# An attention stage put in a fixed order on every engine, with its low parts on GpSimd, its row sums shared with VectorE in PSUM, and its gates and reciprocals taken in at the output chunks

## The chip, the core and the metric

The kernel runs on one core of one Trainium2 chip. The core has TensorE (PE, matrix products, which write PSUM), VectorE (DVE), ScalarE (ACT), GpSimd (POOL, which does not touch PSUM here) and SyncE (SP, whose queue issues nearly all DMAs). Each engine works through its own queue in order and waits on semaphores for the others. The metric is the time of one execution in microseconds (us) on the device; lower is better.

## What is computed

One encoder layer on x of 2048 x 1024 in float32. One projection of x is split between two groups of heads.

```python
h = x @ w_in
g_q, g_k, g_v, g_gate, g_lr_f, g_lr_b, m_cq, m_ckv, m_kr, m_gate = split(h)
o_a = gla_branch(...)                 # 4 heads, gated linear attention, both directions, RMSNorm, * silu(g_gate)
q  = rms_norm(m_cq) @ w_uq            # 4 heads, 128 plain + 64 rotary dims
kv = rms_norm(m_ckv) @ w_ukv          # 4 heads, 128 key dims + 128 value dims, from a latent of 128
s  = (q_nope . k_nope + rope(q_rope) . rope(m_kr)) / sqrt(192)
o_b = softmax(s) @ v * silu(m_gate)   # every query against all 2048 keys
x  = layer_norm(2 ** 0.25 * x + concat(o_a, o_b) @ w_out)
```

## The kernel before, in words

**Precision.** Most products keep near-float32 accuracy by splitting each operand into a high part (float32r, written by a copy on ACT, `hi`, L62) and a low part (operand minus high part, on DVE or GpSimd, `lo`, L69). `mm3` (L80) then takes three matmuls: high x high, high x low, low x high. A plain float32 product is one `matmul` in the source and takes several passes on PE.

**Stages.** `sweep_a` (L304) runs over 16 chunks of 128 rows backwards: the projection for the linear attention, and its backward state. It also makes the tables of the rotary angles, `cos` and `sin`, which lie in the constant pool (L172, L173). `late_gates` (L585) loads the weights of the second sweep, and `sweep_c` (L611) runs over the chunks forwards: the forward state, the latent queries, keys and values, the gates. `setup_q` (L209) also scales the value weights `wv` there. Results that the attention needs go to scratch in DRAM: queries (`qa_s`, `qr_s`), gates (`gm_s`), the linear attention's output (`oa_s`).

**The attention** (`attention`, L894) works in latent space. It loops over 16 blocks (4 ranges of 512 queries x 4 heads), and in a block over 8 pairs of key tiles of 128. A step t of the loop handles the scores of pair t and the values of pair t - 11 (`LEAD` = 3 plus the 8 pairs of a block):

- `s_pair` (L929): ten matmuls put the scores of a pair (two tiles of 128 keys x 512 queries) into a PSUM buffer `pS` of two banks; there are two such buffers. ACT copies them to SBUF (L943), DVE takes the running maximum `rm` over 1024 columns (L948).
- `maxima` (L951), once per block: DVE joins the two halves of `rm`, PE transposes them (`mx`), DVE reduces (`mc`), and PE transposes the result back, spread over 128 rows (`mb`).
- `pv_pair` (L967): DVE subtracts the maximum (L970), ACT takes the exponential (L971), GpSimd adds it to the running sum `acc` (L984), and the values are multiplied into `o`. `PV_MODE` (L46) says how for each of the 8 pairs: `d` makes the low part `pl` on DVE, `p` on GpSimd, `n` takes a plain float32 product with the unsplit values `vf` (L988). A block is `dpdpndpd`; the last two blocks have modes of their own (L47).
- `finish` (L1000): the sum is transposed (`sx`), reduced and inverted on DVE, transposed back (`r`, L1017), multiplied into the output (L1018), the product with `wv` is taken in plain float32 (`y`, L1021), the gate is multiplied in (L1023), and the result goes to scratch `ob_s`.

Buffers are handed out in rings (`tile_pool`), and the framework's list scheduler decides in which order each engine's queue holds the instructions, by priorities from the order in the source.

**The output** (`OutProj`, L1085): `load` (L1107) fetches a chunk of 128 rows of both groups' outputs and splits it (high on ACT, low on GpSimd), 16 x 3 x 2 matmuls per chunk against the split `w_out`, then residual and layer norm on DVE. Chunks 0 and 1 run piecewise (`part`) among the last values; chunks 2 to 15 follow, back to back.

Of the kernel before, what the change touches and what calls it, by code (L numbers as in the profile page):

```python
# [39 lines left out]
W_POOL = (3, 5)  # L40
RND = 1.5 * 2.0 ** 23

PV_MODE = "dpdpndpd"  # L46
PV_LAST = {14: "ddpdnddd", 15: "ddddnddd"}  # L47
# [9 lines left out]
class K:  # L57
# [15 lines left out]
    def after(self, *ins):  # L73

        s = ExitStack()
        for i in ins:
            s.enter_context(self.tc.issue_after(i))
        return s

# [71 lines left out]
    def run(self):  # L151
        tc, nc, ins = self.tc, self.nc, self.ins
        with ExitStack() as top:
# [10 lines left out]
            self.oa_s = [dp.tile([P, H, P], F32, name=f"oa_s{c}") for c in range(NCH)]  # L164
            self.ob_s = [dp.tile([P, H, QB], F32, name=f"ob_s{b}") for b in range(NQB)]
# [5 lines left out]
            self.wv = cp.tile([P, H * P], F32, name="wv")  # L171
            self.cos = cp.tile([P, NCH, 32], F32, name="cosT")  # L172
            self.sin = cp.tile([P, NCH, 2, 32], F32, name="sinT")  # L173
# [27 lines left out]
            self.vf = {k: rp.tile([P, P], F32, name=f"vf{k}") for k in range(NKT) if PV_MODE[k // 2] == "n"}  # L201
# [7 lines left out]
    def setup_q(self, w1, ps):  # L209
# [15 lines left out]
        nc.sync.dma_start(self.wv, ins["wv"])  # L225
# [18 lines left out]
        nc.scalar.activation(self.wv, self.wv, AF.Copy, scale=self.gkv_c[:, 0:1])  # L244
# [48 lines left out]

    def rope_tables(self, hpi):
# [6 lines left out]
        V.tensor_scalar(self.sin[:, :, 0, :], self.sin[:, :, 1, :], -1.0, None, ALU.mult)  # L301


    def sweep_a(self):  # L304
        tc, nc, ins, cp = self.tc, self.nc, self.ins, self.cp
        with ExitStack() as ctx:
# [16 lines left out]
            hpi = wp.tile([P, 1], F32, name="hpi")  # L323
            nc.scalar.preload_act_table_set(EXP_LN)
# [260 lines left out]
    def late_gates(self):  # L585

        tc, nc, ins, bc = self.tc, self.nc, self.ins, self.bc
        self.xch = bc.tile([P, NK, 2, P], F32R, name="xch")
# [229 lines left out]
    def ml_norm(self, d, pm):  # L818
# [12 lines left out]
        ckv = self.vf[c] if c in self.vf else w1.tile([P, P], F32, tag="ckv", name=f"ckv{c}")  # L831
# [6 lines left out]
        if c not in self.vf:  # L838
            self.hi(self.vh[:, c], ckv)
            self.lo(self.vl[:, c], ckv, self.vh[:, c])  # L840
# [53 lines left out]
    def attention(self):  # L894
# [3 lines left out]
        LEAD = 3  # L898
        NP = NKT // 2
        with ExitStack() as ctx:  # L900
            qp = self.wz
            sp = ctx.enter_context(tc.tile_pool(name="sp", bufs=NP + LEAD + 1, reuse_waits="tile"))
            bp = ctx.enter_context(tc.tile_pool(name="bp", bufs=2, reuse_waits="tile"))
            pM = ctx.enter_context(tc.tile_pool(name="pM", bufs=2, space=PSUM, reuse_waits="tile"))
            pO = ctx.enter_context(tc.tile_pool(name="pO", bufs=1, space=PSUM, reuse_waits="tile"))
# [157 lines left out]
            for t2 in sorted(todo):  # L1063
                for fin in todo[t2]:
                    next(fin)
# [171 lines left out]
```

## Time and profile before

| what | value |
|---|---|
| runs (us) | 1402.87, 1403.27, 1405.93; median 1403.27 |
| profiled execution | 1405.04 us, span of its instructions 1403.2 us |
| scores of the attention begin | 671.6 us after the span's start |
| last score matmul | 1186.5 us |
| busy share of the span | PE 95%, DVE 73%, ACT 56%, POOL 49% |
| granted PE clock, mean | 0.983 of full speed |
| share of the chain that ended last | PE 38%, DVE 11%, POOL 10%, ACT 5%, DMA 2% |

In the profile's rows, `L971` is line 971, `s<-s` means tile `s` written from `s`, `x128` the count; then come busy time in us, the mean in ns, and the idle time just before with the engine that ended it. In rows of the timeline the first two numbers are start and duration in us. `PEld` is the loading of weights into PE, `SPq` the issue of DMAs by SP. A matmul's duration includes its way through the array, so matmuls that follow each other overlap in the records, and what one costs is the distance from start to start.

### The profile page before, as it was taken

Reading aid. Unit: us, or ns where it says so; the run is one execution under the profiler, and the core shown is the slowest. Engines: PE = TensorE matmul, PEld = TensorE weight load, DVE = VectorE, ACT = ScalarE, POOL = GpSimd, SP = SyncE. Lnnn points to the kernel's source line nnn. Section 1 sums busy time; section 2 is a strip of 40 time slices with the busy share of each in tenths; the row PEclk is TensorE's granted clock in tenths of the full one; section 3 lists DMA queues with packets and bytes.
Section 4 is the critical chain, followed back from the end, with each engine's and each line's share of the span. In section 5 each row is a group of like instructions: output and inputs, shape, how many; then the busy total and the mean of one; then the engine's idle time right before and its main releaser. Section 6 shows DMA issues by size and latency. Waiting matters only on the chain.

```text
span 1403.2 us, 19420 instructions
## 1 busy us (share of the span) xinstructions
PE 1336.0 (95%) x7072; PEld 1139.4 (81%) x7072; DVE 1021.5 (73%) x1655; ACT 792.1 (56%) x1302; POOL 693.1 (49%) x353
## 2 busy tenths in 40 slices
PE   6899999999989999899999999999999999899997
PEld 6799999999888888888877777777777777678886
DVE  7747764545598777777588888888887789967665
ACT  6555556555565555655566777767666668521100
POOL 2432424232342222231088888888888888662210
PEclk9899999999999999999999999999999999999999
DMA  7222222222565555553821111111111002064432
GB/s 246 87 67 70 66 70 66 71 69 68 178 219 166 173 173 158 173 165 108 270 95 46 46 46 45 45 46 45 45 46 41 20 23 61 16 207 168 143 117 72
DMA packets 85297, 141.56 MB, mean 101 GB/s; under 512 B 9070, under 2 KB 38126, under 8 KB 85200
## 3 DMA queue, kind: packets, MB, share of 16 engines
q1 hardware_dynamic: 84528, 138.21, 31.7%
q0 software_dynamic: 672, 2.10, 0.4%
q8 instruction: 56, 0.92, 0.3%
q14 instruction: 41, 0.34, 0.1%
HBM read 89.95 MB, written 50.33 MB: 100 GB/s over the span
## 4 chain that ended last, share of the span: by engine, by line
PE 38%; DVE 11%; POOL 10%; issue 6%; ACT 5%; DMA 2%; SPq 0%; DVEq 0%; POOLq 0%; ACTq 0%
POOL acc L984 7%; POOL pl L71 3%; DVE MMb L71 2%; PE pS L940 2%; PE pS L941 2%; PE pS L937 2%; PE pS L939 2%; PE pS L938 2%; PE o L83 2%; PE o L84 2%; PE po L82 2%; PE po L84 2%; PE po L83 2%; PE pn L82 2%; PE pn L84 2%
## 5 line engine op out<-in xcount | busy, mean ns | idle before, releaser
L984 POOL TENSOR_TENSOR acc<-acc,s 128x1024 f32<-128x1024 f32 x96 | 269.8, 2811 | 13.4 <-ACT s L971 9.5
L943 ACT ACTIVATE s<-pS 128x1024 f32<-128x1024 f32 x128 | 131.2, 1025 | 108.8 <-PE pS L941 107.3
L970 DVE TENSOR_TENSOR s<-s,mb 128x1024 f32<-128x1024 f32 x128 | 152.9, 1206 | 12.3 <-PE mb L963 12.3
L65 ACT ACTIVATE ph<-s 128x1024 fp32r<-128x1024 f32 x112 | 118.2, 1055 | 44.8 <-PE o L84 44.5
L71 POOL TENSOR_TENSOR pl<-s,ph 128x1024 fp32r<-128x1024 f32 x43 | 109.4, 2544 | 68.4 <-ACT ph L65 68.4
L948 DVE TENSOR_TENSOR rm<-pS,rm 128x1024 f32<-128x1024 f32 x90 | 109.3, 1215 | 40.3 <-ACT s L943 40.3
L82 PE MATMUL ipa<-wah,xah 128*128 128x384 f32 (+1 forms) x384 | 130.8, 341 | 7.0 <-ACT wah L65 7.0
L971 ACT ACTIVATE s<-s 128x1024 f32<-128x1024 f32 x128 | 132.9, 1049 | 5.0 <-DVE s L970 5.0
L71 DVE TENSOR_TENSOR pl<-s,ph 128x1024 fp32r<-128x1024 f32 x69 | 116.3, 1685 | 16.3 <-ACT ph L65 16.1
L84 PE MATMUL ipa<-wah,xal 128*128 128x384 f32 (+1 forms) x384 | 125.9, 328 | 0.0
L83 PE MATMUL ipa<-wal,xah 128*128 128x384 f32 (+1 forms) x384 | 125.5, 327 | 0.2 <-DVE wal L71 0.2
L575 POOL TENSOR_TENSOR Us<-Us,cw 128x512 f32<-128x512 f32 x16 | 18.2, 1138 | 202.0 <-DVE Us L572 172.6
L937 PE MATMUL pS<-qh,ckvT_h 128*128 128x512 f32 x256 | 115.0, 449 | 0.0
L940 PE MATMUL pS<-rh,krs 128*128 128x512 f32 x256 | 101.4, 396 | 0.0
L939 PE MATMUL pS<-qh,ckvT_l 128*128 128x512 f32 x256 | 101.2, 395 | 0.0
L938 PE MATMUL pS<-ql,ckvT_h 128*128 128x512 f32 x256 | 101.0, 395 | 0.0
L941 PE MATMUL pS<-rl,krs 128*128 128x512 f32 x256 | 101.0, 395 | 0.0
L83 PE MATMUL o<-pl,vh 128*128 128x512 f32 x224 | 92.0, 411 | 7.0 <-DVE pl L71 4.0
L82 PE MATMUL o<-ph,vh 128*128 128x512 f32 x224 | 90.3, 403 | 0.8 <-ACT ph L65 0.8
L84 PE MATMUL o<-ph,vl 128*128 128x512 f32 x224 | 89.9, 401 | 0.0
L71 POOL TENSOR_TENSOR ol<-of,oh 128x512 fp32r<-128x512 f32 x32 | 44.5, 1403 | 81.0 <-PE po L84 63.0
L82 PEld LDWEIGHTS ipa<-wah,xah 128*128 128x128 f32 x384 | 73.5, 191 | 7.9 <-ACT wah L65 7.2
(311 smaller groups left out, 3900.4 us busy)
## 6 DMA issues: line engine op xcount, KB each, us to landing
xcf<-xT_dram SPq DMA_DIRECT2D x16, 512.0 KB, 4.0
xr<-x_dram SPq DMA_DIRECT2D x16, 512.0 KB, 3.8
out_dram<-rr SPq DMA_DIRECT2D x32, 256.0 KB, 2.1
xaf<-xT_dram SPq DMA_DIRECT2D x14, 512.0 KB, 4.2
SU<-su_s SPq DMA_DIRECT2D x16, 256.0 KB, 4.1
qdb<-qd_s SPq DMA_DIRECT2D x16, 256.0 KB, 4.5
oib<-oi_s SPq DMA_DIRECT2D x16, 256.0 KB, 2.6
ub<-u_s SPq DMA_DIRECT2D x16, 256.0 KB, 3.0
```

Of the source, the lines that this page charges most:

```text
L71: return e.tensor_tensor(dst, src, hi.bitcast(F32), ALU.subtract).ins
L82: mm(out, ah, bh, start=start, stop=False)
L83: mm(out, ah, bl, start=False, stop=False)
L84: mm(out, al, bh, start=False, stop=stop)
L937: mm(ps[:, e], kh, qh, start=True, stop=False)
L938: mm(ps[:, e], kh, ql, start=False, stop=False)
L939: mm(ps[:, e], kl, qh, start=False, stop=False)
L940: mm(ps[:, e], kr, rh, start=False, stop=False)
L943: d["copy"] = Ac.activation(s, ps, AF.Copy).ins
L970: V.tensor_tensor(s, s, d["mb"][:, None, :].to_broadcast([P, 2, QB]), ALU.subtract)
L971: Ac.activation(s, s, AF.Exp)
L984: d["pool"] = G.tensor_tensor(d["acc"], d["s0"] if j == 1 else d["acc"], s, ALU.add).ins
```

## The change

Line numbers in this section are those of the kernel before, unless said otherwise.

1. A table `PLACE` gives every operation of the attention a place in the order, in units of pairs, and all operations of all blocks are sorted by it (`put`, `todo`). `in_order` chains every instruction of PE, ACT, DVE and POOL to the one before it on its engine, so the scheduler can't change the order. Values now follow the scores by 12 to 13 pairs.
2. All low parts `pl` are made on GpSimd, and no pair takes the plain float32 product: every pair has six value matmuls. `vf` is gone; all 16 value tiles are split.
3. The row sum is shared. DVE adds pairs 0, 1, 2 and 5 half by half (512 columns) into `ap`, a PSUM bank, begun by a copy on ACT; GpSimd adds pairs 3, 4, 6 and 7 into `acc` in SBUF. DVE joins the two (`tot`).
4. The maximum `rm` is kept over 512 columns: two instructions of 512 columns per pair (one for the first pair) take the place of one of 1024, and the joining of the halves goes.
5. The output `o` is split from PSUM (`oh` on ACT, `ol` on DVE) and multiplied unnormalised by `wv`, split too, in three matmuls. The reciprocal is not transposed back; it is stored (`r_s`, 4 bytes an element). Gate and reciprocal are multiplied in when an output chunk is split: two GpSimd multiplications of 512 columns per chunk and two more loads (`gmo`, `ro`).
6. `pM` keeps one bank instead of two; the bank goes to `ap`. `ph` and `pl` get three buffers instead of two. Chunks 2 to 15 take `pM`'s and `pX`'s bank in turn for their first half.
7. `cos` and `sin` leave the constant pool: they are stored to DRAM in the first sweep and read back in `late_gates`; `wv` is loaded, scaled and split at the start of the attention.

The order that results, in a block of the changed kernel's steady state (block 8's scores; places of other engines' instructions as the built program has them):

```
PE    pS8_0  mx7  o6_4  mb7  pS8_1  o6_5  pS8_2  o6_6 o6_7  pS8_3  sx6  pS8_4  o7_0  pS8_5  o7_1  pS8_6  o7_2  pS8_7  o7_3  y6
DVE   mc7 rm0 sub0 sub1 sub2 rm1 sub3 rm2 tot6 ol6 sub4 rm3 ap0 rc6 ap1 rm4 sub5 ap2 rm5 sub6 rm6 ap5 rm7 sub7
ACT   copy0 exp6_7 hi6_7 exp0 copy1 hi0 copy2 exp1 hi1 oh6 exp2 copy3 ap hi2 exp3 copy4 hi3 copy5 exp4 hi4 exp5 copy6 hi5 exp6 copy7 hi6 yc6
POOL  lo0 lo1 lo2 lo3 acc(3,4) lo4 lo5 acc6 lo6 lo7 acc7
```

For chunk 0 (in block 13's values) and chunk 1 (in block 14's) ACT has `oh`0, `oh`1 between `copy4` and `hi3`, and POOL has `ol`0, the two multiplications and `ol`1 between `lo1` and `lo2`. The core of the diff:

```diff
+SUM_DVE = (0, 1, 2, 5)
+SUM_POOL = (3, 4, 6, 7)
+PLACE = dict(copy=0.7, max=1.34,
+    sub=(9.57, 8.73, 7.74, 8.05, 8.32, 8.72, 8.97, 9.57),
++    exp=(9.7, 9.86, 9.37, 9.53, 10.12, 9.46, 9.43, 10.0),
++    hi=(9.91, 10.16, 10.23, 10.53, 10.18, 10.27, 9.71, 10.11),
++    lo=(10.94, 10.28, 11.02, 10.56, 10.41, 10.51, 9.87, 10.58),
++    pv=(12.51, 12.16, 12.85, 12.46, 12.63, 12.87, 12.09, 11.21),
...
+    load=(-11, -3.01),
+    wh=1.83,
+    wl=2.29,
+    part=3.47,
+)
...
+    def in_order(self, last):
...
+        for i in traced[n:]:
+            if i.engine in COMPUTE:
+                if i.engine in last:
+                    self.tc.add_manual_dep(i, last[i.engine].name, mybir.DependencyInfo(
+                        mybir.DependencyClass.NoSync, mybir.DependencyReason.DATA), reason="in_order")
+                last[i.engine] = i
...
+            def smax(i, j):
...
+                    for e in range(2):
+                        V.tensor_tensor(d["rm"], src[:, e], d["rm"], ALU.max)
...
+            def acc(i, j):
+                d = stt[i]
+                s = d["s"][j]
+                if j in SUM_DVE:
+                    for e in range(2):
+                        if j != SUM_DVE[0] or e:
+                            V.tensor_tensor(d["ap"], d["ap"], s[:, e], ALU.add)
...
+            def tot(i):
+                d = stt[i]
+                V.tensor_tensor(d["ap"], d["ap"], d["as"][:, 1], ALU.add)
+                V.tensor_tensor(d["as"][:, 0], d["ap"], d["as"][:, 0], ALU.add)
...
+            def rcp(i):
...
+                nc.sync.dma_start(self.r_s[b][:, h].rearrange("o (e p) -> p (o e)", p=P), rc)
...
+                self.mm3(d["y"], wv_h[:, hs], wv_l[:, hs], d["oh"], d["ol"])
...
+    def split_o(self, o):
...
         for j in range(2):
+            if j:
+                G.tensor_tensor(of[:, 1], of[:, 1], o["gm"], ALU.mult)
+                G.tensor_tensor(of[:, 1], of[:, 1], o["r"], ALU.mult)
...
             kern.hi(oh[j], of[:, j])
             kern.lo(ol[j], of[:, j], oh[j], "pool")
```

For chunks 2 to 15 the split may not be issued before the last instructions of the attention on ACT (`yc` of block 15) and POOL (`acc` of pair 7 of block 15), by `self.after(*pv_end)`; before, it stood behind the last `ph` and the last `acc`.

More of the change, by code (lines that the diff above doesn't have):

```diff
@@ L1000, in finish @@
[L1000 to L1010 removed]
+                    self.mm3(d["o"], self.vh[:, kt], self.vl[:, kt], ph[:, e], pl[:, e],
+                             start=(kt == 0), stop=(kt == NKT - 1))
```

350 lines of the change are left out of this document (202 added, 148 removed).

## The prediction

> **What bounds the kernel now.** I read the page first (busy shares, then the chain), then the busy time by stage, the groups of the attention's steady state, TensorE's instructions in order, and the waits at both ends of the stage.
>
> ```profile
> PE 1336.0 (95%) x7072; PEld 1139.4 (81%) x7072; DVE 1021.5 (73%) x1655; ACT 792.1 (56%) x1302; POOL 693.1 (49%) x353
> 756.71 1.72 PE o L988 x4
> 1154.19 1.72 PE o L988 x4
> 822.94:955.39 132.45, 131.88 (x577) 101.86 (x577) 107.55 (x100) 92.75 (x96) 111.71 (x45) 1.00 0.17 48
> ```
>
> TensorE is busy 95% of the span. The `n` pair recurs every (1154.19 - 756.71) / 12 = 33.12 us, the period of a block (one head, 512 queries). The last row (columns: busy PE, weight loads, DVE, ACT, POOL, then granted clock) holds four periods: PE 131.88 of 132.45, POOL 111.7, DVE 107.6, ACT 92.8, clock 1.00. The chain names GpSimd and others in between, but PE has only 0.57 us without work in four blocks. PE sets the period.
>
> ```profile
> 855.89 1.88 PE L988 MATMUL o<-s,vf 128*128 128x512 f32 x4
> 857.84 0.40 PE L938 MATMUL pS<-ql,ckvT_h 128*128 128x512 f32 x1
> 862.28 0.40 PE L937 MATMUL pS<-qh,ckvT_h 128*128 128x512 f32 x1
> 864.60 0.40 PE L82 MATMUL o<-ph,vh 128*128 128x512 f32 x1
> 877.59 0.60 PE L1017 MATMUL r<-ident,rc 128*128 128x128 f32 x4
> 878.26 0.39 PE L938 MATMUL pS<-ql,ckvT_h 128*128 128x512 f32 x1
> 884.04 0.39 PE L82 MATMUL o<-ph,vh 128*128 128x512 f32 x1
> 884.59 0.50 PE L83 MATMUL o<-pl,vh 128*128 128x512 f32 x1 [0.15 <-POOL pl L71]
> 885.84 1.02 PE L1021 MATMUL y<-osb,wv 128*128 128x512 f32 x2
> 886.93 0.39 PE L938 MATMUL pS<-ql,ckvT_h 128*128 128x512 f32 x1
> ```
>
> Busy times overlap in the array, so I price by start to start. Ten score matmuls take 864.60 - 862.28 = 2.32, that is 0.232 each. Taking off the one L937 that lies between: the `n` pair costs 857.84 - 855.89 - 0.23 = 1.72, four transposes 878.26 - 877.59 - 0.23 = 0.44, the plain fp32 `y` 886.93 - 885.84 - 0.23 = 0.86. A block is 122 x 0.232 + 1.72 + 4 x 0.44 + 0.86 = 32.6; 0.5 is waits, 0.3 of it the wait at 884.59 for a low part made on GpSimd.
>
> **The change, part by part.**
>
> PE per block: the `n` pair becomes six matmuls, `y` becomes three, the transposes of `r` go. 131 x 0.232 + 3 x 0.44 = 31.7, so 0.9 us less work. Whether the waits go too depends on the others:
>
> ```profile
> L984 POOL TENSOR_TENSOR acc<-acc,s 128x1024 f32<-128x1024 f32 x25 | 69.3, 2772 | 2.8 <-ACT s L971 1.8
> L970 DVE TENSOR_TENSOR s<-s,mb 128x1024 f32<-128x1024 f32 x32 | 38.2, 1206 | 3.0 <-PE mb L963 3.0
> L971 ACT ACTIVATE s<-s 128x1024 f32<-128x1024 f32 x32 | 33.2, 1047 | 0.0
> L943 ACT ACTIVATE s<-pS 128x1024 f32<-128x1024 f32 x32 | 32.8, 1026 | 28.1 <-PE pS L941 28.1
> L71 POOL TENSOR_TENSOR pl<-s,ph 128x1024 fp32r<-128x1024 f32 x12 | 30.7, 2557 | 1.0 <-ACT ph L65 1.0
> L65 ACT ACTIVATE ph<-s 128x1024 fp32r<-128x1024 f32 x28 | 29.6, 1056 | 10.1 <-PE o L84 10.1
> L1006 POOL TENSOR_TENSOR acc<-acc 128x512 f32<-128x512 f32 x4 | 5.2, 1292 | 0.3
> L1023 DVE TENSOR_TENSOR gma<-y,gma 128x512 f32<-128x512 f32 x4 | 2.8, 692 | 0.6 <-PE y L1021 0.5
> L1012 DVE TENSOR_REDUCE rc<-sx 128x4 f32<-128x512 f32 x4 | 2.7, 674 | 0.0
> L1004 ACT ACTIVATE osb<-o 128x512 f32<-128x512 f32 x4 | 2.4, 600 | 1.5 <-PE o L84 1.5
> 871.54 2.41 POOL L71 TENSOR_TENSOR pl<-s,ph 128x1024 fp32r<-128x1024 f32 x1 [0.24 <-ACT ph L65]
> ```
>
> POOL: eight low parts and three sums. No DVE instruction of a block reads two SBUF tensors any more (one side is always PSUM), and beside such ones a low part took 2.41: 11 x 2.41 = 26.5 (by the means above, 28.4). ACT: 8 x (1.026 + 1.047 + 1.056) + 3 x 0.60 = 26.8. DVE: eight subtractions 9.65; 15 half maxima, 7 half sums, 2 totals and the subtraction of `ol` at 0.69, 17.3; two reductions 1.35: 28.3. All stay under 31.7, but DVE with only 3 us.
>
> So I laid one block out by hand along the changed kernel's order, zero at the end of the `mx` transposes, each maximum behind the copy of its scores (it waits for that by its semaphore). Scores of pairs 1 to 7 end on PE at 4.2, 7.9, 13.0, 15.7, 19.4, 23.1, 26.9. ACT copies pair 5 by 20.7, DVE ends its maxima at 24.1, and pair 7 wants that buffer at 24.5: 0.4 us of slack, the tightest place. GpSimd has each low part 3.7 to 5.6 us before its matmul. So PE goes on setting the period, and I take 31.8 (31.7 to 32.3): 13 periods, from the end of block 2's scores to the end of block 15's (756.7 to 1186.75, below, = 430.0), become 413.4: **-16.6**.
>
> The one price with no row is a DVE instruction that writes PSUM (`ap`). From below it is 0.67 (the 512-element reduction), from above 1.21, the row of twice its length. I take 0.69, the nearest in shape. The Trainium skill, PSUM — Partial Sum Buffer, Specifications (TRN2), gives VectorE 1.04 ns per 4-byte element written there, an estimate of 0.53 us plus a start for 512. By it this term stays at 0.69; no run here shows it.
>
> Start of the stage:
>
> ```profile
> L937 PE MATMUL pS<-qh,ckvT_h x256: 387/396/797, 671.6 to 1185.6; 128*128 128x512 f32 x128
> L941 PE MATMUL pS<-rl,krs x256: 387/393/628, 672.6 to 1186.5; 128*128 128x512 f32 x128
> 720.00:730.00 10.00, 7.15 (x24) 5.56 (x23) 6.39 (x6) 3.47 (x4) 9.64 (x5) 0.66 0.11 38
> ```
>
> Scores begin at 671.6 and end at 1186.5 + 0.23. Block 2's end 85.1 after the start, for 24 x 2.32 + 11 x 1.39 + 1.72 + 6 x 0.44 + 0.86 = 76.2 of work (a value pair is six matmuls, 1.39); the rest, 8.9, is idle time and a cold clock (the slice at 720 shows 0.66). In the new order the same stretch holds 24 score pairs, 11 value pairs and 5 transpose groups (73.2), and my layout finds 3.6 us of waits, 1.6 of them behind block 0's maxima: 76.8, **-8.3**.
>
> The two early output chunks now cost. Each is split in the middle of a block: ACT makes `oh`0, GpSimd `ol`0, then the two new multiplications, and ACT's next instruction is `oh`1, which waits for them; behind it on ACT stand the high part of pair 3 and a score copy, and on GpSimd the low part of pair 2.
>
> ```profile
> L71 POOL TENSOR_TENSOR ol<-of,oh 128x512 fp32r<-128x512 f32 x32 | 44.5, 1403 | 81.0 <-PE po L84 63.0 <-ACT oh L65 8.5 <-DMA out_dram<-rr 6.6
> L65 ACT ACTIVATE oh<-of 128x512 fp32r<-128x512 f32 x32 | 19.8, 629 | 71.0 <-PE po L84 55.1 <-DMA of<-oa_s 11.0 <-DMA of<-ob_s 4.7
> 1221.56 0.79 PE L83 MATMUL o<-pl,vh 128*128 128x512 f32 x1 [4.00 <-DVE pl L71]
> 1220.00:1230.00 10.00, 8.44 (x25) 5.71 (x26) 9.96 (x8) 6.35 (x6) 6.35 (x4) 0.83 0.15 51
> ```
>
> ACT comes to it at 17.9 of the layout: + 0.63 + 1.40 + 2 x 1.29 + 0.63 + 1.40 + 2.41, handshakes 0.4 (the 0.24 at 871.54 holds one) = 27.4, where PE wants that low part at 23.4: 4.0 us idle. After the idle 4.00 at 1221 the slice shows clock 0.83, 1.7 us lost. Twice (4.0 + 1.7): **+11.4** (0 if the cover held, 16 with the loss at 0.66). The Trainium skill, TensorE: Matmul & The Clock Gate, What's actually happening, says that an idle window of about 3.4 us halves the clock until as long has been busy; by it the loss is 1.7 a time, and for a stall below 3.4 nothing.
>
> The end:
>
> ```profile
> 1194.12 1.12 PE L958 MATMUL mx<-ident,rm 128*128 128x128 f32 x4 [2.98 <-DVE rm L955]
> L71 DVE TENSOR_TENSOR wol<-wof,woh 128x1024 fp32r<-128x1024 f32 x6 | 13.6, 2269 | 0.7 <-POOL wol L71 0.6
> 1203.83 3.11 POOL L984 TENSOR_TENSOR acc<-s,s 128x1024 f32<-128x1024 f32 x1 [1.04 <-ACT s L971]
> 1393.38 0.39 PE L82 MATMUL po<-woh,oh 128*128 128x512 f32 x1
> 1394.51 0.39 PE L84 MATMUL po<-woh,ol 128*128 128x512 f32 x1
> ```
>
> Before: from the last score (1186.75) to the last matmul (1394.74) 208.0, with idle 2.98 and 4.00. After: GpSimd has 20 instructions left at the last score (12 low parts and six sums of blocks 14 and 15, two low weights) and paces the end: 20 x 2.41 = 48.2; I take 50, since beside DVE's low weights, with two SBUF inputs and 2.27 long, one took 3.11. Then two totals, transposes, `y`: +3.2, and chunk 2's split, which may not start before `yc` of block 15: 0.60 + 0.63 + 1.40 + 0.5 = 3.1. The 672 matmuls of chunks 2 to 15 at (1394.51 - 1393.38) / 5 = 0.226 are 152. Sum 208.5: **+0.5** (-2 to +5). In chunks 2 to 15 GpSimd's 2 x 1.40 + 2 x 1.29 = 5.4 lies beside 10.9 of PE; the extra DMAs of gates and reciprocals are issued two chunks ahead on SP, behind loads that wait for the residual of three chunks before.
>
> Earlier stages:
>
> ```profile
> 380.00:400.00 20.00, 20.00 (x102) 17.30 (x101) 16.14 (x24) 17.29 (x31) 5.64 (x6) 1.00 0.70 241
> 390.02 0.33 SPq L758 DMA_DIRECT2D SU<-su_s  x1
> 397.73 0.63 ACT L65 ACTIVATE MMb<-SU 64x512 fp32r<-64x512 f32 x1
> ```
>
> `cosC` and `sinC` (768 KB) go on SP ahead of three weight loads and of the first state `SU`, at the start of the second sweep: 3 us at the 241 GB/s of that stretch. `SU` was issued at 390.0 and first read at 397.7, which hides most of it: **+0.5** (0 to 2). The scaled `wv` and the reciprocals' stores hide beside PE.
>
> Sum: -16.6 - 8.3 + 11.4 + 0.5 + 0.5 = -12.5 on the profiled run's own 1405.04 (span 1403.2, 1.8 around it): 1392.5. The median of the runs shown is 1.8 below that run, so **1391**.
>
> **The rivals.**
>
> DVE paces the block (slower). Six PSUM-writing instructions stand between pair 2's maxima and the place with 0.4 of slack. Each extra e delays PE by 6e - 0.4 in 14 blocks; the gain of 12 us is used up at e = 0.21, so from 0.91 us an instruction the kernel is slower. At 1.0 the block gains 1.4: 20 us, 1411; at 1.21, 1429. For it: no row has such a write, and the fixed order lets no engine work ahead. Against: those that read it run at the usual length (0.69 for half of 1.21).
>
> The fixed order gains nothing. Were each pair's handshakes 0.11 us later than I allow, 8 x 14 x 0.11 = 12: 1403.
>
> The splits are covered. If PE meets the low part in time, the 11.4 goes: 1380. Against it stands the order of ACT and GpSimd.
>
> **How the numbers follow.** Forecast 1391 (1384 to 1398) 0.55; splits covered 0.14; nothing gained 0.08; DVE paces 0.23. For 8 in 10 the range takes in 1380 and DVE pacing up to 1.0 us an instruction: 1378 to 1412. About 0.2%, 2.8 us, is what a measurement can tell from no change: faster 0.69, same 0.07, slower 0.24.
>
> **What would show it.** Right: a period of 31.8 in the order of PE, no idle time before `o` in blocks 3 to 12, POOL's low parts near 2.41, two idle gaps of about 4 us in the blocks where `oh0_0` and `oh1_0` stand, a gap of 3 us ahead of chunk 2. Wrong: PE waiting for scores' buffers with DVE as releaser, `ap` instructions over 0.9 us, a period above 32.5.

## The result, and the profile after

| what | before | changed |
|---|---|---|
| median of the runs of the first measurement (us) | 1405.03 (5 runs) | 1394.42 (5 runs, 1392.28 to 1397.97) |
| ratio, 95% interval | | 0.993 (0.9911 to 0.995) |
| second measurement, on another occasion | 1404.95 | 1397.20 (6 runs, 1391.73 to 1402.35), ratio 0.9946 (0.9926 to 0.9966) |
| profiled execution, span of its instructions | 1405.04, 1403.2 | 1397.97, 1396.2 |

The change is faster by 0.5 to 0.7%. The profiled execution of the changed kernel is the slowest of its five runs, 3.55 us above their median; keep that in mind when its terms are compared with the forecast.

The page of the changed kernel, busy us with the share of the span, then two of its groups (busy us and mean ns ahead of the second bar), and last a stretch of a little over four blocks (columns as in the prediction):

```profile
PE 1317.6 (94%) x7056; PEld 1141.4 (82%) x7056; DVE 1041.9 (75%) x1828; ACT 825.4 (59%) x1353; POOL 721.7 (52%) x391
...
L98 POOL TENSOR_TENSOR pl<-s,ph 128x1024 fp32r<-128x1024 f32 x128 | 308.3, 2418 | 79.2 <-ACT ph L92 52.1
L1053 DVE TENSOR_TENSOR ap<-ap,s 128x512 f32<-128x512 f32 x112 | 77.5, 692 | 1.7
872.00:1004.00 132.00, 132.00 (x597) 107.46 (x596) 112.87 (x151) 106.37 (x114) 110.40 (x47) 1.00 0.15 41
```

All 128 low parts now stand on GpSimd, at 2.42 us where twelve of before took 2.56. A DVE instruction that adds into PSUM takes 692 ns; it was the one price without a row, and 0.69 had been taken. In the stretch from 872 to 1004 PE is busy for all of 132.00 us; in four blocks of before it was without work for 0.57.

The lines by which the stage divides, from PE's timeline (start and duration in us, and in brackets the idle time just before with what ended it):

```profile
749.23 0.39 PE L984 MATMUL pS<-rl,krs 128*128 128x512 f32 x1
753.84 0.60 PE L1008 MATMUL mx<-ident,rm 128*128 128x128 f32 x4
1102.54 0.60 PE L1008 MATMUL mx<-ident,rm 128*128 128x128 f32 x4
1129.51 0.79 PE L125 MATMUL o<-pl,vh 128*128 128x512 f32 x1 [2.95 <-POOL pl L98]
1165.97 0.50 PE L125 MATMUL o<-pl,vh 128*128 128x512 f32 x1 [2.97 <-POOL pl L98]
1170.89 0.40 PE L984 MATMUL pS<-rl,krs 128*128 128x512 f32 x1
1190.47 0.80 PE L125 MATMUL po<-wol,oh 128*128 128x512 f32 x1 [6.41 <-DVE wol L98]
1229.67 0.47 PE L124 MATMUL y<-ofh,wv_h 128*128 128x512 f32 x1 [2.21 <-DVE rc L1086]
1231.82 0.80 PE L124 MATMUL pn<-woh,oh 128*128 128x512 f32 x1 [1.21 <-ACT oh L92]
1249.12 0.50 PE L126 MATMUL pn<-woh,ol 128*128 128x512 f32 x1 [1.14 <-POOL ol L98]
1387.30 0.39 PE L126 MATMUL po<-woh,ol 128*128 128x512 f32 x1
```

Scores begin at 671.64, as before. Block 2's end at 749.23 + 0.23 = 749.46, block 15's at 1170.89 + 0.23 = 1171.12. From 753.84 to 1102.54 lie eleven periods: (1102.54 - 753.84) / 11 = 31.70, which is the bare sum of the matmuls, 131 x 0.232 + 3 x 0.44 = 31.71. So each step can be measured:

| step | before | changed | difference | in the second profile | forecast |
|---|---|---|---|---|---|
| earlier stages | 671.6 | 671.64 | 0 | +1.9 | +0.5 |
| start, to the end of block 2's scores | 85.1 | 749.46 - 671.64 = 77.8 | -7.3 | -8.7 | -8.3 |
| 13 periods | 430.0 | 13 x 31.70 = 412.1 | -17.9 | -17.9 | -16.6 |
| the two early splits | 0 | 1171.12 - 749.46 - 412.1 = 9.6 | +9.6 | +8.1 | +11.4 |
| end, last score to last matmul | 208.0 | 1387.53 - 1171.12 = 216.4 | **+8.4** | **+7.8** | +0.5 |
| after the last matmul | 8.5 | 8.7 | +0.2 | +0.2 | 0 |
| sum | 1403.2 | 1396.2 | -7.0 | -8.7 | -12.5 |

The second profile is one of the changed kernel again, taken in the second measurement (1396.26 us, span 1394.5). Its terms are read in the same way: scores from 673.49, block 2's end at 749.89, eleven periods of 31.70, block 15's end at 1170.06, the last matmul's at 1385.82.

Everything up to the last score came out within 3.3 us a step, mostly on the good side. The end is 7 to 8 us over its forecast, more than the whole difference between forecast and result.

It helps to set the end beside that of the kernel before, where PE has this:

```profile
1239.73 0.48 PE L82 MATMUL pn<-woh,oh 128*128 128x512 f32 x1
1243.44 1.13 PE L1021 MATMUL y<-osb,wv 128*128 128x512 f32 x2 [0.84 <-DVE osb L1018]
```

From the last score to the last block's `y` it is 56.9 us there, 58.8 in the changed kernel and 56.6 in its second profile. From that `y` to the last matmul it is 151.1 there, 157.6 and 159.2 here (all from start to start). Before, chunk 2 had begun ahead of the last `y` (nine matmuls from 1239.73 on, 2.0 us of work), so PE waited only 0.84 for it. Now chunk 2 comes behind it, with idle time on both sides (2.21 and 1.21 in the rows above), and chunk 3 waits another 1.14. So 6.5 of the 8.4, and all of the second profile's 7.8, come from the last `y` on.

### The profile page after: what moved, and what is told of

Same layout as the page of the kernel before. It is cut to its first block, busy times and chain, and to the rows that moved or that the text cites. A ratio compares the mean times of both kernels' runs of the same rounds, so it can differ in the third digit from the quotient of the medians.

```text
span 1396.2 us, 19855 instructions
## 1 busy us (share of the span) xinstructions
PE 1317.6 (94%) x7056; PEld 1141.4 (82%) x7056; DVE 1041.9 (75%) x1828; ACT 825.4 (59%) x1353; POOL 721.7 (52%) x391
## 5 line engine op out<-in xcount | busy, mean ns | idle before, releaser
L98 POOL TENSOR_TENSOR pl<-s,ph 128x1024 fp32r<-128x1024 f32 x128 | 308.3, 2418 | 79.2 <-ACT ph L92 52.1
L1002 DVE TENSOR_TENSOR rm<-pS,rm 128x512 f32<-128x512 f32 x210 | 144.9, 690 | 50.3 <-ACT s L989 45.6
L989 ACT ACTIVATE s<-pS 128x1024 f32<-128x1024 f32 x128 | 131.0, 1024 | 80.2 <-PE pS L984 70.9
L92 ACT ACTIVATE ph<-s 128x1024 fp32r<-128x1024 f32 x128 | 135.5, 1059 | 17.8 <-PE o L126 16.0
L126 PE MATMUL ipa<-wah,xal 128*128 128x384 f32 (+1 forms) x384 | 126.0, 328 | 0.0
L125 PE MATMUL o<-pl,vh 128*128 128x512 f32 x256 | 102.1, 399 | 8.4 <-POOL pl L98 8.4
L980 PE MATMUL pS<-qh,ckvT_h 128*128 128x512 f32 x256 | 104.7, 409 | 2.2 <-ACT s L989 1.9
L124 PE MATMUL o<-ph,vh 128*128 128x512 f32 x256 | 102.6, 401 | 0.0
L126 PE MATMUL o<-ph,vl 128*128 128x512 f32 x256 | 101.9, 398 | 0.0
L92 ACT ACTIVATE oh<-of 128x512 fp32r<-128x512 f32 x32 | 19.0, 625 | 110.7 <-POOL of L1240 102.3
L1053 DVE TENSOR_TENSOR ap<-ap,s 128x512 f32<-128x512 f32 x112 | 77.5, 692 | 1.7
L1058 POOL TENSOR_TENSOR acc<-acc,s 128x1024 f32<-128x1024 f32 x32 | 78.1, 2442 | 0.0
```

Of the source, the lines that this page charges most:

```text
L92: return nc.scalar.activation(dst, src, AF.Copy).ins
L98: return e.tensor_tensor(dst, src, hi.bitcast(F32), ALU.subtract).ins
L124: mm(out, ah, bh, start=start, stop=False)
L125: mm(out, ah, bl, start=False, stop=False)
L126: mm(out, al, bh, start=False, stop=stop)
L980: mm(ps[:, e], kh, qh, start=True, stop=False)
```

## The experiments

All kernels are edits of the changed kernel unless said otherwise. Each expectation names its theories A and B for that run alone. "S to N" below is the time from the start of the last score matmul to the first matmul of chunk 2, "N to E" from there to the last matmul, both by start times from one profiled execution; in the changed kernel they are 60.9 and 155.5, in its second profile 59.2 and 156.6; from the first score to the last it is 499.3 and 496.3.

**What the fixed order is worth.** The chaining goes, everything else stays; the scheduler orders the queues again.

```diff
-                with self.in_order(last):
-                    fn(*a)
+                n = len(nc.cur_bb.bb.instructions)
+                fn(*a)
+                for i in nc.cur_bb.bb.instructions[n:]:
+                    last[i.engine] = i
```

> The fixed order alone is undone: all instructions as in the changed kernel, but each engine's order is left to the planner, which moves maxima, sums and transposes against one another; the sums still go through PSUM. Theory A, that the order itself is worth what the waits of before were (0.5 us a block) and at most 0.6 more: the period rises from 31.7 to 32.2 to 32.8, 7 to 18 us more, 1401 to 1412. Rival B, that the order gains nothing and the period comes from TensorE's smaller work alone: 31.7 to 31.8, 1393 to 1397.

Measured: 1411.08 (1407.55 to 1416.04), ratio to before 1.0057 (1.0037 to 1.0077). Three successive `mx` of its steady state:

```profile
825.11 0.60 PE L1008 MATMUL mx<-ident,rm 128*128 128x128 f32 x4
857.48 0.60 PE L1008 MATMUL mx<-ident,rm 128*128 128x128 f32 x4
889.83 0.60 PE L1008 MATMUL mx<-ident,rm 128*128 128x128 f32 x4
```

(889.83 - 825.11) / 2 = 32.36 a block, where the fixed order has 31.70: it is worth 0.66 a block, some 9 us in 14 blocks, and the stretch from first to last score is 509.9. Theory A had this right. Without the order the rest of the change is slower than the kernel before, by 0.4 to 0.8%. This also answers the rival "the fixed order gains nothing": it gains.

**Where the sums lie.** DVE's running sum goes to an SBUF tile in place of the PSUM bank.

```diff
-                d["ap"] = pA.tile([P, QB], F32, tag="ap", name=f"ap{i}")
+                d["ap"] = qp.tile([P, QB], F32, tag="wz", name=f"ap{i}")
```

> VectorE's running sum lies in SBUF in place of PSUM, so that its seven half sums a block read and write SBUF alone; order and work are the same. Theory A, that an instruction of VectorE with two SBUF operands and GpSimd's instructions keep each other waiting: the half sums (0.69 us now) take 1.2 to 2.5 us, GpSimd's low parts rise from 2.42 to over 2.55, VectorE goes from 28 to over 33 us a block, and the period rises by 2 to 6 us, 1425 to 1475. Rival B, that the place of the sum does not matter: half sums 0.6 to 0.7 us, period 31.7, 1393 to 1397.

Measured: 1532.28 (1528.89 to 1537.52), ratio 1.0921 (1.09 to 1.0942). From its page and PE's timeline:

```profile
L98 POOL TENSOR_TENSOR pl<-s,ph 128x1024 fp32r<-128x1024 f32 x128 | 332.7, 2602 | 145.9 <-ACT ph L92 124.2
L1053 DVE TENSOR_TENSOR ap<-ap,s 128x512 f32<-128x512 f32 x112 | 228.7, 2042 | 1.7
842.99 0.47 PE L980 MATMUL pS<-qh,ckvT_h 128*128 128x512 f32 x1 [2.43 <-DVE rm L1002]
```

The same addition takes 2042 ns with both inputs in SBUF and 692 with one in PSUM, and its output stands in the same place as that input. Seven of them a block are 7 x 1.35 = 9.5 us more DVE, which had 4.6 to spare (112.87 busy of 132.00 in the stretch shown above, 27.1 of 31.70 in a block); PE now waits for scores' buffers behind the maxima, and 137.9 us are lost against the changed kernel's first median, 8.6 a block. The Trainium skill, SBUF — State Buffer, Who interferes with whom, says that a DVE instruction with two SBUF inputs contends with a GpSimd instruction that reads SBUF, since its second input comes through the port pair that the two engines share. The 2042 beside GpSimd's 2602 agree; what this run shows is that the change needs the bank of PSUM.

**How much DVE has to spare.** Pair 4's two maxima are taken twice in every block but the first, 2 x 0.69 = 1.38 us of DVE at the place that the layout had called tightest.

```diff
+                        if j == 4 and i:
+                            V.tensor_tensor(d["rm"], src[:, e], d["rm"], ALU.max)
```

> In every block but the first the two half maxima of pair 4 are made twice (same result): VectorE has 1.38 us more ahead of the maximum of pair 5. Theory A, the prediction's layout, which leaves VectorE 0.4 us at that place: TensorE waits 1.0 us a block for the scores' buffer, 14 us more, 1406 to 1410. Theory B, the changed kernel's trace, where that maximum ends 1.0 us ahead of its use: 0.4 us a block, 1398 to 1402. Rival C, that VectorE is nowhere near the path: no change, 1393 to 1397.

Measured: 1406.15 (1403.60 to 1410.16), ratio 1.0026 (1.001 to 1.0042).

```profile
840.44 0.47 PE L980 MATMUL pS<-qh,ckvT_h 128*128 128x512 f32 x1 [0.35 <-DVE rm L1004]
872.85 0.47 PE L980 MATMUL pS<-qh,ckvT_h 128*128 128x512 f32 x1 [0.35 <-DVE rm L1004]
```

The period is 872.85 - 840.44 = 32.41, so 1.38 us of DVE cost 0.71 of PE: the slack was 0.67, not 0.4 and not the 1.0 that the trace had suggested. PE paces the block, but two more maxima on DVE, 5% of its 27 us a block, take the whole gain of the change back. The rival "DVE paces the block" was this near; it fell on the price of `ap` alone.

**The stall of 6.41 us at the end.** In the changed kernel's profile PE waits 6.41 us for the first of DVE's low weights, which took 10.12 us. DVE's and GpSimd's timelines there:

```profile
1180.29 10.12 DVE L98 TENSOR_TENSOR wol<-wof,woh 128x1024 fp32r<-128x1024 f32 x1
```

```profile
1177.59 4.77 POOL L98 TENSOR_TENSOR pl<-s,ph 128x1024 fp32r<-128x1024 f32 x2
1182.28 2.43 POOL L1058 TENSOR_TENSOR acc<-acc,s 128x1024 f32<-128x1024 f32 x1
1184.63 4.70 POOL L98 TENSOR_TENSOR pl<-s,ph 128x1024 fp32r<-128x1024 f32 x2
1195.70 2.41 POOL L98 TENSOR_TENSOR pl<-s,ph 128x1024 fp32r<-128x1024 f32 x1 [6.38 <-ACT ph L92]
```

GpSimd's instructions lie back to back until 1184.63 + 4.70 = 1189.33, and DVE's ends 1.08 later, at 1190.41. It stood still until GpSimd had nothing to do. Then GpSimd stood still itself, for 6.38 us (last row), by way of ACT:

```profile
1194.05 0.60 ACT L1045 ACTIVATE ap<-s 128x512 f32<-128x512 f32 x1 [7.54 <-DVE acc L1073]
```

ACT's copy that begins the next sum waited for DVE's total, which stood behind the low weight on DVE, and the high part that GpSimd needed stood behind this copy on ACT. In the first experiment on it GpSimd's next instruction waits for DVE's low weight, so that DVE gets in:

```diff
+    def yields(self, i):
+        for w in self.held:
+            self.k.tc.add_manual_dep(i, w.name, mybir.DependencyInfo(
+                mybir.DependencyClass.Sync, mybir.DependencyReason.DATA), reason="yields")
+        self.held = []
...
-                self.lo(d["pl", j], d["s"][j], d["ph", j], "pool")
+                op.yields(self.lo(d["pl", j], d["s"][j], d["ph", j], "pool"))
...
-                    G.tensor_tensor(d["as"], d["as"], s, ALU.add)
+                    op.yields(G.tensor_tensor(d["as"], d["as"], s, ALU.add).ins)
```

> At the end of the attention the next GpSimd instruction in the order waits (semaphore) for each low part of the output weights that VectorE makes; nothing else is changed. Theory A, that VectorE's first such low part (two SBUF operands, 10.12 us long in the changed kernel's profile, TensorE idle 6.41 us behind it) is kept out by GpSimd instructions that run back to back: with GpSimd held it takes 1.2 to 2.5 us, the idle time of 6.41 falls under 2, and the time falls by 3 to 8 us, to 1386 to 1391. Rival B, that this low part is late for its own weights or for VectorE's queue: its length and the idle time stay, and the six waits add up to 6 x 1.3 = 8 us, 1394 to 1402.

Measured: 1395.77 (1389.13 to 1397.63), ratio 0.9936 (0.9918 to 0.9954). The low weight took 4.25 us, GpSimd stood 1.23 for it, and the stall went:

```profile
1178.92 4.25 DVE L98 TENSOR_TENSOR wol<-wof,woh 128x1024 fp32r<-128x1024 f32 x1
```

```profile
1228.68 0.80 PE L124 MATMUL pn<-woh,oh 128*128 128x512 f32 x1 [1.21 <-ACT oh L92]
```

Yet S to N went from 60.9 to 59.6 only, and the time can't be told from that of the changed kernel. The low weight came as soon as GpSimd was held, as theory A has it; but A's 3 to 8 us were not gained. The unchanged kernel, run again:

> The changed kernel itself beside the three others, and a second profile of it. Theory A, that VectorE's first low weight is kept out by GpSimd's run of instructions in every execution: again 9 to 11 us long with 6 to 7 us of idle time on TensorE, and 1392 to 1397. Rival B, that it was an accident of the one profiled execution, which was the slowest of five: 2 to 3 us long, no idle time there, and 4 to 6 us less from the last score to chunk 2.

Measured: 1397.20 (1391.73 to 1402.35), ratio 0.9946 (0.9926 to 0.9966). In this execution DVE's low weight wasn't held up; a GpSimd instruction was a little longer in its place:

```profile
1179.70 1.91 DVE L98 TENSOR_TENSOR wol<-wof,woh 128x1024 fp32r<-128x1024 f32 x1
```

```profile
1183.80 3.39 POOL L1058 TENSOR_TENSOR acc<-acc,s 128x1024 f32<-128x1024 f32 x1
...
1219.40 2.39 POOL L1058 TENSOR_TENSOR acc<-acc,s 128x1024 f32<-128x1024 f32 x1
```

So the stall is not there in every execution: theory A fell, and rival B was right on the low weight and on the idle time, but not on its 4 to 6 us. GpSimd's last sum ends at 1221.79, and the last score 51.7 us before; with the stall it was 53.97, and S to N was 1.8 longer.

What the stall is worth is more than that, since the last score is not a fixed mark. In the first profile the clock fell behind the second early split (0.85 in the slice from 1160, 1.00 in the second profile), and the last score came 1.5 us later for it, while GpSimd went on. From the same `mx` ahead of both splits (1102.54, and 1102.97 in the second profile) to chunk 2 it is 129.3 and 126.0. In the profile of a run below that is the same kernel up to chunk 3's loads (the one without the additional loads, where the low weight took 3.15 us) it is 125.5. So 6.4 us of idle time on PE were worth 3.3 to 3.8.

The rest came back on GpSimd. Beside each of DVE's six low weights one GpSimd instruction takes 3.4 us instead of 2.4: six of them in the second profile. In the first it is three, since DVE finished three low weights while GpSimd stood idle. Its idle time there, 6.38 and 0.38, less 3 x 1.0 leaves 3.8. In the second profile GpSimd's queue of 20 instructions runs without a pause from the last score to the last sum: this queue paces the stretch.

**Relieving that queue.** In block 15, DVE takes all eight pairs' sums (a copy on DVE puts the total into SBUF), so GpSimd has three instructions fewer.

```diff
+                d["dve"] = tuple(range(NP)) if i == nb - 1 else SUM_DVE
...
-                if j in SUM_DVE:
+                if j in d["dve"]:
...
+                if i == nb - 1:
+                    d["as"] = bp.tile([P, 2, QB], F32, tag="acc", name=f"acc{i}", bufs=1)
+                    V.tensor_copy(d["as"][:, 0], d["ap"])
+                    return
```

> The three sums that GpSimd makes in the last block (2.4 us each) are made by VectorE in PSUM, as six half sums of 0.69; nothing else is changed. Theory A, that from the last score to the last low part GpSimd's queue sets the pace and not the 6.41 us that TensorE waits for VectorE's first low weight: the stretch from the last score to chunk 2's first matmul (60.7 us in the changed kernel's profile, 59 without the 6.41) shrinks by 5 to 7 us, 1387 to 1390. Rival B, that VectorE's chain (low weights, sums, totals) is as late as GpSimd's: less than 2 us are gained, 1392 to 1397.

Measured: 1390.36 (1386.63 to 1394.93), ratio 0.9897 (0.9879 to 0.9916); the unchanged change on the same chip 0.9946 (0.9926 to 0.9966). The intervals are apart.

```profile
1222.36 0.50 PE L124 MATMUL pn<-woh,oh 128*128 128x512 f32 x1 [1.20 <-ACT oh L92]
```

S to N is 54.2, five us less than in the second profile of the change, taken beside it, where the first low weight took 1.91 us as it did here. Theory A holds, with a median 0.4 us above its range: GpSimd's queue sets the start of chunk 2.

**The two early splits.** The four steps of each split (`oh`0 and `ol`0; gate; reciprocal; `oh`1 and `ol`1) are spread over three pairs, and the second is put at the same place of the next block, so that no `oh`1 stands in ACT's queue ahead of its input.

```diff
+SPLIT = (("0", 0.03), ("g", 0.6), ("r", 1.5), ("1", 2.9))
...
-                put(NP * nb + PLACE["load"][c], split, c)
+                for s, dt in SPLIT:
+                    put(NP * nb + PLACE["load"][0] + 8 * c + dt, split, c, s)
```

> The splits of output chunks 0 and 1 are cut in four steps that stand apart in the order: first half behind low part 2, the two multiplications behind low part 3 and low part 4, second half behind low part 6. The work is the same. Theory A, that the two stalls (2.95 and 2.97 us, with 1.8 us of cold clock each) come from where the steps stand, ScalarE being held 4.0 us by its second half and low part 2 being queued behind all of it: both stalls go, 9.5 us less, about 1385. Rival B, that GpSimd's 5.2 us of added work exceed its 4.9 us of slack in a block wherever they stand: idle time of 2 to 3 us moves to a later low part of the same block, 1391 to 1395.

Measured: 1392.71 (1387.57 to 1395.02), ratio 0.9919 (0.9904 to 0.9935). ACT's and GpSimd's timelines of the changed kernel show what was undone, and then the slices of ten us in the two kernels (columns as in the prediction, the granted clock third from the end):

```profile
1125.15 0.63 ACT L92 ACTIVATE oh<-of 128x512 fp32r<-128x512 f32 x1 [4.03 <-POOL of L1240]
```

```profile
1127.09 4.71 POOL L98 TENSOR_TENSOR pl<-s,ph 128x1024 fp32r<-128x1024 f32 x2
```

```profile
1130.00:1140.00 10.00, 10.00 (x41) 8.02 (x41) 5.77 (x9) 6.85 (x8) 10.00 (x5) 0.86 0.28 58
```

```profile
1120.00:1130.00 10.00, 10.00 (x45) 8.15 (x44) 7.91 (x11) 7.47 (x9) 10.00 (x6) 1.00 0.35 26
```

ACT stood 4.03 us at `oh`1, the low part behind it on GpSimd came at 1127.09, PE waited 2.95 for it, and the following slice shows a clock of 0.86. In the experiment (last row) the stalls are gone and the stretch from first to last score falls to 491.1. But S to N rises to 62.7: GpSimd has the same work, PE reaches it sooner, and of 8.2 us saved 1.8 are gone by chunk 2 (against the second profile 5.3 are saved and 3.5 gone; but here the first low weight took 9.03 us, as in the first). The medians differ by 1.7, and the intervals overlap. So the cause of the stalls is as theory A has it, and the time is in rival B's range, though the idle time of 2 to 3 us that B expected ahead of a later low part isn't there (only 0.66 and 0.94, behind DVE). Both cures together:

```diff
+SPLIT = (("0", 0.03), ("g", 0.6), ("r", 1.5), ("1", 2.9))
...
+                d["dve"] = tuple(range(NP)) if i == nb - 1 else SUM_DVE
```

> Two of the edits together, with SyncE's order as in the changed kernel: the early splits in four steps apart, and the last block's sums on VectorE. Theory A, that both are separate costs: 4 to 6 us less than the sums alone (1390.4), 1384 to 1387. Rival B, that what the splits save on TensorE is given back because GpSimd's queue, with the same work, sets when chunk 2 begins: 1389 to 1392.

Measured: 1388.87 (1383.10 to 1391.76), ratio 0.9902 (0.9875 to 0.9928). That can't be told from the sums alone (0.9897). First to last score is 491.1, S to N 60.7, with the lock-out of 9.04 us in this profile. It is the lowest median, 0.4% below the unchanged change's first one, and it beats the kernel before by 0.7 to 1.25%.

**Chunk 3's gates.** In the changed kernel PE waits again at 1249.12, for a low part of chunk 3. GpSimd and the DMA queue of SP there:

```profile
1243.61 1.29 POOL L1239 TENSOR_TENSOR of<-of,gmo 128x512 f32<-128x512 f32 x1 [7.36 <-DMA gmo<-gm_s]
```

```profile
1220.82 7.87 SPq L1249 DMA_DIRECT2D xr<-x_dram  x4
...
1232.13 0.52 SPq L1226 DMA_DIRECT2D gmo<-gm_s  x1
```

The issue of four residual loads took SP 7.87 us, since they waited for buffers. The gates stood behind them, and behind the two stores of the last block (issued at 1230.23 and 1231.28). First, the work stays and the gates of chunks 2 and 3 are loaded ahead of the loop; in the same edit every later split is chained in order on ACT and GpSimd, not only behind the attention's last instructions:

```diff
+            two = [op.load(c) for c in (2, 3)]
...
-                    with self.after(*pv_end):
+                    with self.in_order(pv_end):
```

> The gates and reciprocals of chunk 3 are issued on SyncE ahead of the four loads for the residual, which hold SyncE 7.9 us, and the splits of chunks 2 and 3 stand in order; nothing else is changed. Theory A, that chunk 3 waits for its late gates because of SyncE's order: GpSimd's wait for that transfer (7.36 us) and TensorE's 1.14 us in chunk 3 go, 152 to 154 us in place of 155.7 from chunk 2's first matmul to the last, 1391 to 1393. Rival B, that the transfers themselves are slow (reciprocals stored in 4-byte pieces): the wait stays, 1393 to 1397.

Measured: 1404.53 (1401.11 to 1408.93), ratio 1.0006 (0.9993 to 1.0019): worse than the change by 7 to 10 us, which neither theory had. Chunk 3's gates are in time, but six later chunks wait. GpSimd, ACT, DVE and PE at one of them:

```profile
1326.73 1.29 POOL L1241 TENSOR_TENSOR of<-of,ro 128x512 f32<-128x512 f32 x1 [8.02 <-DMA ro<-r_s]
```

```profile
1328.05 0.63 ACT L92 ACTIVATE oh<-of 128x512 fp32r<-128x512 f32 x1 [12.35 <-POOL of L1241]
1328.81 0.20 ACT L136 ACTIVATE ln_y<-ln_l 128x1 f32<-128x1 f32 x1
```

```profile
1329.05 1.02 DVE L137 TENSOR_TENSOR ln_t<-ln_y 128x1 f32<-128x1 f32 x1 [4.47 <-ACT ln_y L136]
```

```profile
1334.76 0.47 PE L124 MATMUL pn<-woh,oh 128*128 128x512 f32 x1 [2.67 <-DVE rr L1276]
```

A reciprocal is late, so `oh` of a chunk not needed yet holds ACT for 12.35 us; the layer norm's `ln_y` of 0.20 us stands behind it, DVE behind that, and PE waits for the PSUM bank that DVE empties with the residual. It is the mechanism of the early splits once more: a late input on an engine that works in order. The edit changes two things at once, so this run doesn't price the earlier loads by themselves. Two more kernels carry the same order with the other cures; the second has the residual's loads of chunks 4 to 15 on ACT's queue:

```diff
+            two = [op.load(c) for c in (2, 3)]
...
+SPLIT = (("0", 0.03), ("g", 0.6), ("r", 1.5), ("1", 2.9))
...
+                d["dve"] = tuple(range(NP)) if i == nb - 1 else SUM_DVE
...
+                if fn is oh:
+                    pv_end = {e: last[e] for e in (mybir.EngineType.Activation, mybir.EngineType.Pool)}
```

> Four edits together: the splits of chunks 0 and 1 in four steps apart, the last block's sums on VectorE, chunk 3's gates loaded first, and chunk 2's split ahead of the last y instead of behind its copy. Theory A, that these are separate costs on the path: 6 (splits) + 6 (sums) + 2 (gates) + 4 (chain of sx, reciprocal, y, copy ahead of chunk 2) = 18 us less than the changed kernel's 1394, about 1376 (1372 to 1381). Rival B, that one limit stands behind them all (VectorE's low weights held up by GpSimd): under 8 us less, 1386 to 1392.

```diff
-        self.nc.sync.dma_start(o["xr"], self.k.ins["x"][c * P:(c + 1) * P].rearrange("p (a d) -> p a d", a=2))
+        q = self.nc.scalar if c > 3 else self.nc.sync
+        q.dma_start(o["xr"], self.k.ins["x"][c * P:(c + 1) * P].rearrange("p (a d) -> p a d", a=2))
```

> The four edits of the run that came out at 1398, with one more: from chunk 4 on the load for the residual is issued on ScalarE's queue instead of SyncE's. Theory A, that TensorE's waits for VectorE's residual in that run (eight, 0.9 to 2.7 us, 12 us in all) came from these loads standing behind stores and gates on SyncE: the waits go, 152 to 155 us from chunk 2's first matmul to the last in place of 168.5, 1380 to 1386. Rival B, that the transfers themselves are at their limit with 512 KB more a chunk: waits of 6 us or more remain, 1391 to 1398.

Measured: 1398.22 (1396.97 to 1401.73), ratio 0.9957 (0.9944 to 0.997), and 1408.26 (1401.66 to 1414.51), ratio 1.0043 (1.0023 to 1.0062). N to E is 168.3 and 182.1, against 155.5. All four theories missed: taking the residual loads off SP made it worse still. From the second kernel's ACT, DVE and PE:

```profile
1263.41 0.63 ACT L92 ACTIVATE oh<-of 128x512 fp32r<-128x512 f32 x1 [6.59 <-POOL of L1249]
1263.95 0.18 ACT L136 ACTIVATE ln_y<-ln_l 128x1 f32<-128x1 f32 x1
```

```profile
1264.17 1.26 DVE L137 TENSOR_TENSOR ln_t<-ln_y 128x1 f32<-128x1 f32 x1 [7.13 <-ACT ln_y L136]
```

```profile
1270.08 0.67 PE L124 MATMUL pn<-woh,oh 128*128 128x512 f32 x1 [4.05 <-DVE rr L1287]
```

The layer norm's `ln_y` again stands behind an `oh` whose input is late. GpSimd's waits for reciprocals add up to 63.8 us in this profile, 51.0 in that of the first kernel and 28.9 in the changed kernel's. Why they come later with the residual's loads on ACT's queue isn't shown.

One thing the pair does show: up to chunk 2 the two kernels have the same order, and S to N is 57.6 with a first low weight of 8.95 us in one and 51.4 with 1.22 in the other. Where GpSimd's queue has been relieved, the lock-out costs about six us; where it has not, 3.3 to 3.8.

**What the additional loads cost.** Chunks 3 to 15 take chunk 2's gates and reciprocals, so their loads go (and the output is another).

```diff
+        if c > 2:
+            nc.sync.dma_start(of[:, 1], kern.ob_s[b][:, :, cs])
+            return dict(c=c, of=of, gm=self.gm2, r=self.r2)
```

> Chunks 3 to 15 use the gates and reciprocals of chunk 2: 13 x 2 loads of 256 KB are left out, the multiplications stay (so the output of these chunks is another). Theory A, that these loads make up the excess of the output stage (155.7 and 156.8 us from chunk 2's first matmul to the last, 152 by its matmuls): 152 to 154 us, 1390 to 1394. Rival B, that the excess is the cold clock after the 3.4 us of idle time ahead of chunk 2, which no load causes: 155 us or more, 1394 to 1397.

Measured: 1392.37 (1389.49 to 1394.68), ratio 0.9932 (0.9908 to 0.9955).

```profile
1226.54 0.50 PE L124 MATMUL pn<-woh,oh 128*128 128x512 f32 x1 [1.21 <-ACT oh L92]
...
1380.76 0.39 PE L126 MATMUL po<-woh,ol 128*128 128x512 f32 x1
```

N to E is 154.2, for 155.5 and 156.6 in the two profiles of the change. Of some 4 us over the 152 laid out, the loads make up 1.3 to 2.4 by these two, and the wait of 1.14 in chunk 3 (1.19 in the second profile) is gone; the result lies between the theories. Five other profiles with these loads and the changed kernel's order in this stretch show 156.2 to 158.3, so it may be up to 4. The rest goes with a cold clock, which this slice of the changed kernel shows behind the idle 2.21 and 1.21 ahead of chunk 2:

```profile
1230.00:1240.00 10.00, 8.79 (x31) 6.46 (x30) 9.99 (x22) 2.86 (x8) 4.40 (x3) 0.83 0.94 94
```

At 0.83 ten us lose 1.7.

## Why the prediction came out as it did

**What bounds the kernel: right.** PE set the period before and sets it after. The signs that were named show: no idle time on PE in the stretch from 872 to 1004, low parts at 2.42, two idle gaps at the splits and 2.21 + 1.21 ahead of chunk 2. The period is the sum of the matmuls to 0.01 us; 31.8 had been taken for a few handshakes that don't show. Two experiments stand behind it: without the fixed order a block is 0.66 longer, and 1.38 us more of DVE lengthens the block by 0.71. The slack of 0.4 in the layout was 0.67, so the layout was on the cautious side by 0.3.

**Step 1, thirteen periods, -16.6: right**, measured -17.9. The price of a DVE instruction that writes PSUM was 0.69 against 692 ns measured.

**Step 2, the start, -8.3: right**, measured -7.3 and -8.7.

**Step 3, the splits, +11.4: right in mechanism**, measured 9.6. The stalls were 2.95 and 2.97 instead of 4.0 (in the trace ACT came to `oh`0 half a us earlier than laid out, and a split on GpSimd took 1.28 to 1.29, not 1.40). What is left, 9.6 - 5.9 = 3.7, is 1.8 a time for the cold clock, as forecast; in the second profile, with the same stalls, it is 2.1, since only the first was followed by a cold clock (0.83 in that slice, 1.00 behind the second). The upper bound of 16 was summed wrongly: at a clock of 0.66 ten us lose 3.4, and 2 x (4.0 + 3.4) is 14.8. The forecast's sentence that by the Trainium skill, TensorE: Matmul & The Clock Gate, What's actually happening, a stall below 3.4 us would cost nothing did not hold here: after 2.95 the next slice shows 0.86.

**Step 4, the end, +0.5: the step that failed**, measured +8.4, beyond its own bounds of -2 to +5. Three terms of it were too small, and the forecast was 208.5 against 216.4 (the terms as written add up to 208.3):

- GpSimd to its last sum: 50 taken, 53.97 measured, 51.7 in the second profile. The queue was named rightly and its instructions counted rightly. But DVE's six low weights lengthen six of them by 1.0 each, where 1.8 had been allowed in all; this is what the second profile shows. In the first it is three of them, and GpSimd is idle for 6.76 behind the low weight that was locked out, which the prediction did not have.
- From there to chunk 2: 6.3 taken, 6.7 and 7.2 measured.
- Chunks 2 to 15: 152 taken, 155.7 and 156.8 measured. Two things were left out. PE's idle time ahead of chunk 2 was counted as waiting, but not the cold clock after it (1.7), though the same price had been charged at the splits. And that the extra DMAs are issued behind loads that wait was written down without asking when they would come: chunk 3's gates came 7.36 us late for GpSimd, and the loads cost 1.3 to 2.4 in all by the two profiles of the change.

**Step 5, earlier stages, +0.5:** measured 0 and +1.9, inside its 0 to 2; no run here tells the added loads from what varies between executions.

**The sum.** 1392.5 was forecast on the scale of the profiled run and 1397.97 measured: +1.0 - 1.3 - 1.8 + 7.9 - 0.5 + 0.2 = 5.5. On the scale of the medians it is 1391 against 1394.42 and 1397.20. (The terms are those of steps 2, 1, 3, 4, 5 and the tail, and 7.9 is 8.4 - 0.5.) The errors of steps 1 and 3 hid 3 us of the error of step 4. That is luck: with those two steps as forecast, the two medians would have been 1397.5 and 1400.3, at the range's upper end of 1398 and beyond it.

**The rivals.** "DVE paces the block" fell by its own criterion (0.69, not over 0.91), but the last run of that kind shows how little was missing. "The fixed order gains nothing" fell. "The splits are covered" fell: both stalls are there, and the kernel without them, at a median of 1392.71, does not reach 1380, and GpSimd's queue takes a part of what is saved back at the end.

**What stays open.** Of the thirteen profiles of the changed kernel and its edits, DVE's first low weight was held up 9 to 10 us in four and took 1.2 to 4.3 in the others, the same kernel among both; why DVE gets in at one boundary between GpSimd's instructions and not at the next three isn't settled. Nor has an earlier load of the gates been tried with the old order on ACT. And no run undoes the six value matmuls, the split `y` or the move of `cos` and `sin` alone: what the first two are worth is read from the matmuls' distances.

## What to carry to other kernels

Where a stage ends, count the instructions left in the queue of each engine before pricing the stalls that can be seen: a wait of 6.4 us on PE was worth 3.3 to 3.8, since GpSimd, with 50 us of work left, got part of it back, while three instructions less on GpSimd were worth 5. An engine that works in order makes a wait of everything behind the waiting instruction, also of the short one that another engine needs, so a step whose input comes late is put where its input is sure to be there. And an idle gap of about 3 us ahead of TensorE is priced by its length and by the cold clock that may follow it.

## What the runs showed of the hardware

- An idle gap of 2.95 us was followed by a clock of 0.86 in the next ten us, and 2.21 and 1.21 with three matmuls between them by 0.83. The Trainium skill, TensorE: Matmul & The Clock Gate, What's actually happening, puts the idle window at about 3.4 us; these gaps are shorter. It wasn't so each time: behind the second split's stall of 2.97 the first profile of the changed kernel shows 0.85 in the slice from 1160 and the second 1.00.
- DVE's low weight with two SBUF inputs took 1.91 in one execution and 10.12 in another at the same place of the same kernel; where it got in, a GpSimd instruction took 3.39 instead of 2.39.
- With one input and the output in PSUM in place of SBUF, DVE's addition of 512 columns took 692 instead of 2042 ns beside a busy GpSimd.
